# A two-layer hybrid trunk in split float32: matmuls that read and write their columns backwards, and an input tile moved to a multiple of 128 bytes

## The chip, the core and the metric

The kernel runs on one core of a Trainium2 chip. The metric is the device time of one execution in microseconds (us). One execution was also taken by the hardware profiler; all views shown here are of it. Engines: PE is TensorE's matmul side, PEld its weight load, DVE is VectorE, ACT is ScalarE, POOL is GpSimd, SP issues the DMAs.

## The reference

A decoder trunk of two layers on 256 tokens of 1024 channels, in float32. Each layer is a half-step SwiGLU FFN, a token mixer, and a second half-step FFN.

```python
h = x
for l in range(2):
    h = h + 0.5 * swiglu(rms_norm(h, ffn1_norm[l]), ffn1_w_in[l], ffn1_w_out[l])   # 1024 -> 2 x 2816 -> 1024
    u = rms_norm(h, mix_norm[l])
    (z_s, xbc, dt_s, qkv, z_d, b_d, a_d, gate_s, gate_d) = split(u @ w_in[l])      # 1024 -> 11312
    y_s = mamba2_branch(...)                # convolution, chunked state-space scan, gated norm
    y_d = deltanet_branch(...)              # convolution, chunked delta rule, gated norm
    merged = sigmoid(gate_s) * (y_s @ ssm_w_branch[l]) + sigmoid(gate_d) * (y_d @ dn_w_branch[l])
    h = h + merged @ w_out[l]
    h = h + 0.5 * swiglu(rms_norm(h, ffn2_norm[l]), ffn2_w_in[l], ffn2_w_out[l])
return rms_norm(h, final_norm)
```

## The kernel before

All large weights stream from HBM as 504 halves of 128 x 1024 floats (`load`, tile `wraw`, five buffers). ACT rounds each half to the type float32r (`whi`, line 60 through `act`), DVE subtracts (`wlo`, line 63 through `tt`); five split halves are kept. The other operand of a weight matmul is split in the same way, and a product is the sum of three matmuls in float32r: high by high, high by low, low by high. Two helpers issue those three, `mm3` (lines 208 to 211) and `mm3w` (213 to 216):

```python
PE.matmul(ps, lh, rh, start=start, stop=False)      # sum, stationary operand, moving operand
```

The second argument is the stationary operand, which is loaded into the array ahead (PEld); the third is the moving one, whose columns are streamed through; the first is the sum in PSUM, a float32 column for each moving column.

The normalised input is transposed once a norm into `uTh` and `uTl` (128 partitions, 8 blocks of 256 tokens each), high and low part. They stand in the pool `cpool`, which holds its tiles for the whole run. Weight matmuls come in three kinds:

- `chan_chunk`, by `mm3w`: the weight half is stationary (128 x 128), `uTh` or `uTl` moves with 256 columns. The sums are called `fc` in the FFNs, `kk`, `qq`, `vv`, `zd`, `bc`, `xs` in the mixer. `psm` (line 391, `scalars`) is of the same kind, with a stationary operand of 48 columns (`wsh`, `wsl`).
- `tok_chunk`, by `mm3`: a slice of `uTh` or `uTl` is stationary (128 x 128), the weight half moves with 512 columns. Sums: `f` in the FFNs, `t` in the mixer.
- `out_chunks`, by `mm3`: a slice of a split activation is stationary, the weight half moves with 512 columns. Sums: `o` (stationary `gh`, `gl` in the FFNs, `mh`, `ml` after the mixer) and `b` (stationary `bh`, `bl`, the branches).

All other matmuls (transposes, the chunked parts of the mixer) are issued directly and not through these helpers.

The order of the work is the program's order of calls (`ORDER` in the mixer) with a scheduler that places instructions by priority; the weights' order in HBM is the order in which `take` is called.

Tiles lie in SBUF one behind another within a pool. In the built program of before the tiles of `cpool` begin: `h` at byte 16512 of each partition (a multiple of 128), `cs` 24704, `mhalf` 28288, `one` 28320, `Y0` 28832, `Y1` 30880, `uTh` 32928, `uTl` 41120, `nw` 49312, `lp` 53408. So the 4-byte tile `mhalf` (with its padding 32 bytes) puts `uTh` and `uTl` 32 bytes past a multiple of 128. `wraw`, `whi`, `wlo`, `gh`, `gl`, `mh`, `ml`, `bh`, `bl` begin at multiples of 128; `wsh` and `wsl` too, with slices that begin at 0 or 64 past one.

Of the kernel before, what the change touches and what calls it, by code (L numbers as in the profile page):

```python
# [7 lines left out]
F32 = mybir.dt.float32  # L8
# [8 lines left out]
P = 128  # L17
# [8 lines left out]
LPW = 48 * 5 + 16 + 1  # L26
# [19 lines left out]
def trunk_kernel(ctx, tc, x, wst, wsm, norms, lpar, rpar, cst, out):  # L46
    nc = tc.nc
    V, A, G, PE = nc.vector, nc.scalar, nc.gpsimd, nc.tensor

    cpool = ctx.enter_context(tc.tile_pool(name="cpool", bufs=1))  # L50
# [3 lines left out]
    sm = ctx.enter_context(tc.tile_pool(name="sm", bufs=1))  # L54
# [51 lines left out]
    def ahead(key, n, fn):  # L106
        while state[key] < min(n, n_halves):
            fn(state[key])
            state[key] += 1
# [35 lines left out]
    LIMT = cs[:, 3 * P + 64 : 4 * P]  # L145
    SEL = [cs[:, 4 * P : 5 * P], cs[:, 5 * P : 6 * P]]
    LAST = cs[:, 6 * P : 7 * P]
    mhalf = cpool.tile([P, 1], F32, name="mhalf")
    V.memset(mhalf[:], -0.5)

    one = cpool.tile([1, P], F32, name="one")
# [39 lines left out]
    def norm_in(nw, add=None):  # L191

        for t in range(2):
# [4 lines left out]
            if t == 0:  # L198
# [6 lines left out]
                with tc.issue_after(ins.ins):  # L205
                    ahead("prepped", n + 2, prep)

    def mm3(ps, lh, ll, rh, rl, start, stop):
        PE.matmul(ps, lh, rh, start=start, stop=False)  # L209
        PE.matmul(ps, lh, rl, start=False, stop=False)  # L210
        PE.matmul(ps, ll, rh, start=False, stop=stop)  # L211

    def mm3w(ps, wh, wl, mh, ml, start, stop):
        PE.matmul(ps, wh, mh, start=start, stop=False)  # L214
        PE.matmul(ps, wh, ml, start=False, stop=False)  # L215
        PE.matmul(ps, wl, mh, start=False, stop=stop)  # L216

    def tok_chunk(ps, ks):

        ws = [(k, take()) for k in ks[::2]]  # L220
        for t in range(2):
            for k0, (wh, wl) in ws:
                for k in range(2):
                    kt = k0 + k
                    mm3(
                        ps[t][:],
                        uTh[:, kt, t * P : (t + 1) * P],
                        uTl[:, kt, t * P : (t + 1) * P],
                        wh[:, k * 512 : (k + 1) * 512],
                        wl[:, k * 512 : (k + 1) * 512],  # L230
                        kt == 0,
                        kt == KT - 1,
                    )

    def chan_chunk(ps):

        ws = [take(), take()]
        for a in range(2):
            for q in range(2):
                wh, wl = ws[q]  # L240
                for k in range(4):
                    kt = 4 * q + k
                    c0 = k * 256 + a * P
                    mm3w(
                        ps[:, a * 256 : (a + 1) * 256],
                        wh[:, c0 : c0 + P],
                        wl[:, c0 : c0 + P],
                        uTh[:, kt, :],
                        uTl[:, kt, :],
                        kt == 0,  # L250
                        kt == KT - 1,
                    )

    def out_chunks(ps, stat, ks, last, group=1, split=False):

        for g0 in range(0, len(ks), group):
            kk = ks[g0 : g0 + group]
            ws = [(k, take()) for k in kk]
            for t in range(2):
                order = [(k, n) for n in range(2) for k in range(len(kk))]  # L260
                if t == 1 and not split:
                    order = [(k, n) for k in range(len(kk)) for n in range(2)]
                for k, n in order:
                    k, (wh, wl) = ws[k]
                    sh, sl = stat(k, t)
                    mm3(
                        ps[t][n][:], sh, sl,
                        wh[:, n * 512 : (n + 1) * 512], wl[:, n * 512 : (n + 1) * 512],
                        k == 0, k == last,
                    )  # L270
# [58 lines left out]

    def mixer(l, nxt):  # L330
        with tc.issue_after(state["last"].ins):
            lp = cpool.tile([P, LPW], F32, tag="lp", name="lp")
            nc.sync.dma_start(lp[:], lpar[l])
            rp = cpool.tile([P, RPW], F32, tag="rp", name="rp")
            nc.sync.dma_start(rp[:], rpar[l].partition_broadcast(P))
            wsr = s2.tile([P, KT, 48], F32, tag="s2", name="wsr")
            nc.sync.dma_start(wsr[:], wsm[l])
# [51 lines left out]
        def scalars():  # L389
            psm = trb("psm")  # L390
            for kt in range(KT):
                mm3w(psm[0:48, 0:S], wsh[:, kt, :], wsl[:, kt, :], uTh[:, kt, :], uTl[:, kt, :], kt == 0, kt == KT - 1)
# [518 lines left out]
        def branch(kind, n, mk, tail=1):  # L911
            ps = [[accb("b"), accb("b")] for _ in range(2)]
            held = {}

            def stat(k, t):
                oh, ol = held[k // 2]
                return oh[:, k % 2, t * P : (t + 1) * P], ol[:, k % 2, t * P : (t + 1) * P]

            made = 1
            for j0 in list(range(n - tail)) + [n - tail]:  # L920
                js = range(j0, j0 + (tail if j0 == n - tail else 1))
                while made < min(js[-1] + 2, n):
                    mk(made)
                    made += 1
                for j in js:
                    held[j] = brT.pop((kind, j))
                out_chunks(ps, stat, [2 * j + i for j in js for i in range(2)], 2 * n - 1, group=2 * len(js))
            return ps
# [56 lines left out]
        m = tg[1]  # L985
        ps = branch("s", 8, ss_T)
        mh = slots.tile([P, KT, S], F32R, tag="sE", name="mh")
        ml = slots.tile([P, KT, S], F32R, tag="sH", name="ml")
# [26 lines left out]
    for l in range(DEPTH):  # L1015
        ffn(norm_vec(3 * l + 1))
        mixer(l, norm_vec(3 * l + 2))
        add = ffn(norm_vec(3 * l + 3) if l + 1 < DEPTH else None)
# [131 lines left out]
```

## Time and profile before

| | |
|---|---|
| median of 3 runs | 1595.85 us (1595.24 to 1600.74) |
| the profiled execution, its own time | 1593.43 us |
| its span, first to last instruction | 1591.6 us |
| granted TensorE clock | 0.999 |
| instructions | 28859, of which 11672 matmuls and as many weight loads |
| moved by DMA | 284.73 MB, mean 179 GB/s |

The profile's groups give, for each line, operation and shape, the busy time in us, the mean duration of one in ns, and the idle time of the engine before them. Matmuls overlap in the pipeline: a matmul that the groups show with 279 ns can follow the one before it after less than half of that. What a matmul costs in a dense row is therefore read from the timeline, from the start of one to the start of a later one, divided by the number of steps between them.

### The profile page before, as it was taken

To read this page: it belongs to the slowest core of one execution; us is meant where nothing else is said; L and a number is where in the kernel's file an instruction comes from. 1 tells how busy PE (TensorE), PEld (TensorE's weight loads), DVE (VectorE), ACT (ScalarE), POOL (GpSimd) and SP (SyncE) were. 2 spreads that over 40 slices of the span, in tenths; PEclk is the share of its full clock that TensorE was granted. 3 is DMA by queue.
4 is the path that set the end of the run, shared out by engine and by line. 5 is a ranking of instruction groups with operands and counts; after the bars stand their busy time and mean duration, and the time that the engine had idled before them with its cause. 6 is when DMAs were issued, how large, how long until landed. Compare 5 with 4: busy or idle time off the path is not lost.

```text
span 1591.6 us, 28859 instructions
## 1 busy us (share of the span) xinstructions
PE 1572.3 (99%) x11672; PEld 1420.9 (89%) x11672; DVE 1069.1 (67%) x1550; ACT 880.1 (55%) x1416; POOL 58.1 (4%) x60
## 2 busy tenths in 40 slices
PE   8999999999999999999999999999999999999998
PEld 7999879999888888999899987899998888889986
DVE  5555468957899766555465555698579996675554
ACT  5444468756565654444354444686656665454443
POOL 0000020000000000000000001000000000000000
PEclk9999999999999999999999999999999999999999
DMA  7555465543465456555565565655436555555562
GB/s 268 193 188 195 161 203 192 166 149 117 173 214 172 159 170 189 188 192 190 173 207 190 186 196 174 197 176 180 129 120 207 178 170 175 172 175 194 187 196 96
DMA packets 91915, 284.73 MB, mean 179 GB/s; under 512 B 22069, under 2 KB 23045, under 8 KB 90758
## 3 DMA queue, kind: packets, MB, share of 16 engines
q1 hardware_dynamic: 91782, 282.90, 54.8%
q8 instruction: 91, 1.49, 0.4%
q14 instruction: 42, 0.34, 0.1%
HBM read 280.94 MB, written 1.92 MB: 178 GB/s over the span
## 4 chain that ended last, share of the span: by engine, by line
PE 91%; DVE 4%; DMA 2%; ACT 1%; POOL 1%; issue 0%; SPq 0%; POOLq 0%; ACTq 0%
PE fc L216 9%; PE fc L214 9%; PE fc L215 9%; PE o L211 6%; PE o L209 5%; PE o L210 5%; PE t L209 4%; PE t L210 3%; PE t L211 3%; PE b L211 3%; PE b L210 2%; PE b L209 2%; PE xs L215 2%; PE xs L214 2%; PE xs L216 2%; DVE wlo L63 1%
## 5 line engine op out<-in xcount | busy, mean ns | idle before, releaser
L63 DVE TENSOR_TENSOR wlo<-wraw,whi 128x1024 fp32r<-128x1024 f32 x504 | 613.6, 1223 | 376.4 <-ACT whi L60 369.3
L60 ACT ACTIVATE whi<-wraw 128x1024 fp32r<-128x1024 f32 x504 | 531.0, 1060 | 429.3 <-PE fc L215 176.2
L214 PE MATMUL fc<-uTh,whi 128*128 128x256 f32 x1280 | 357.4, 279 | 0.0
L215 PE MATMUL fc<-uTl,whi 128*128 128x256 f32 x1280 | 357.0, 279 | 0.0
L216 PE MATMUL fc<-uTh,wlo 128*128 128x256 f32 x1280 | 357.0, 279 | 0.0
L215 PEld LDWEIGHTS fc<-uTl,whi 128*128 128x128 f32 x1280 | 240.6, 188 | 0.2
L214 PEld LDWEIGHTS fc<-uTh,whi 128*128 128x128 f32 x1280 | 240.6, 188 | 0.2
L216 PEld LDWEIGHTS fc<-uTh,wlo 128*128 128x128 f32 x1280 | 240.6, 188 | 0.0
L209 PE MATMUL o<-whi,gh 128*128 128x512 f32 x352 | 137.3, 390 | 0.0
L210 PE MATMUL o<-wlo,gh 128*128 128x512 f32 x352 | 137.3, 390 | 0.0
L211 PE MATMUL o<-whi,gl 128*128 128x512 f32 x352 | 137.0, 389 | 0.0
L209 PE MATMUL t<-whi,uTh 128*128 128x512 f32 x256 | 103.2, 404 | 1.0 <-ACT uTh L60 1.0
L210 PE MATMUL t<-wlo,uTh 128*128 128x512 f32 x256 | 101.6, 397 | 0.0
L211 PE MATMUL t<-whi,uTl 128*128 128x512 f32 x256 | 101.1, 396 | 0.0
L211 PEld LDWEIGHTS o<-whi,gl 128*128 128x128 f32 x352 | 66.1, 188 | 13.8
L210 PEld LDWEIGHTS o<-wlo,gh 128*128 128x128 f32 x352 | 66.1, 188 | 13.6
L209 PEld LDWEIGHTS o<-whi,gh 128*128 128x128 f32 x352 | 66.1, 188 | 13.4
L209 PE MATMUL b<-whi,bh 128*128 128x512 f32 x192 | 76.3, 399 | 0.0
L210 PE MATMUL b<-wlo,bh 128*128 128x512 f32 x192 | 74.9, 390 | 0.0
L211 PE MATMUL b<-whi,bl 128*128 128x512 f32 x192 | 74.3, 394 | 0.6 <-DVE bl L63 0.6
L214 PE MATMUL xs<-uTh,whi 128*128 128x256 f32 x256 | 73.1, 286 | 0.0
L216 PE MATMUL xs<-uTh,wlo 128*128 128x256 f32 x256 | 71.6, 280 | 0.0
(259 smaller groups left out, 2915.6 us busy)
## 6 DMA issues: line engine op xcount, KB each, us to landing
wraw<-in_wst_dram SPq DMA_DIRECT2D x504, 512.0 KB, 4.3
dc<-rdram SPq DMA_DIRECT2D x8, 1024.0 KB, 9.2
nw<-in_norms_dram SPq DMA_DIRECT2D x6, 512.0 KB, 4.9
gb<-rdram SPq DMA_DIRECT2D x8, 256.0 KB, 6.1
h<-in_x_dram SPq DMA_DIRECT2D x4, 256.0 KB, 3.1
out_dram<-fo SPq DMA_DIRECT2D x4, 256.0 KB, 2.3
dq<-X SPq DMA_DIRECT2D x2, 256.0 KB, 4.8
cs<-in_cst_dram SPq DMA_DIRECT2D x1, 384.0 KB, 8.2
```

The lines of the kernel that those rows point to most:

```text
L60: return A.activation(out=o, in_=i, func=func, **kw)
L63: return V.tensor_tensor(out=o, in0=a, in1=b, op=op)
L209: PE.matmul(ps, lh, rh, start=start, stop=False)
L210: PE.matmul(ps, lh, rl, start=False, stop=False)
L211: PE.matmul(ps, ll, rh, start=False, stop=stop)
L214: PE.matmul(ps, wh, mh, start=start, stop=False)
L215: PE.matmul(ps, wh, ml, start=False, stop=False)
L216: PE.matmul(ps, wl, mh, start=False, stop=stop)
```

## The change

A helper `mm` gives a matmul the same columns in reverse: the moving operand is read from its last column to its first (step -1), and the sum is written from its last column to its first, so that each column's result lands where it did. The stationary operand is read as before. All matmuls of `mm3` and `mm3w` go through it; the other matmuls stay as they are.

`mhalf` moves from `cpool` into the pool `sm`. With that, `uTh` begins at byte 32896 and `uTl` at 41088, both multiples of 128. `lp` grows from 257 to 272 columns (its DMA writes 257 as before), which takes up the 32 bytes: `rp`, `wsh`, `wsl` and all tiles of the pools for weights and activations lie where they lay. In `sm`, the small tiles move up by 32 bytes.

The order of instructions on each engine is the same in both programs, with the same DMAs.

```diff
-    mhalf = cpool.tile([P, 1], F32, name="mhalf")
+    mhalf = sm.tile([P, 1], F32, name="mhalf", bufs=1)
...
+    def mm(ps, w, m, start, stop):
+
+        PE.matmul(ps[:, ::-1], w, m[:, ::-1], start=start, stop=stop)
+
     def mm3(ps, lh, ll, rh, rl, start, stop):
-        PE.matmul(ps, lh, rh, start=start, stop=False)
-        PE.matmul(ps, lh, rl, start=False, stop=False)
-        PE.matmul(ps, ll, rh, start=False, stop=stop)
+        mm(ps, lh, rh, start, False)
+        mm(ps, lh, rl, False, False)
+        mm(ps, ll, rh, False, stop)
 
     def mm3w(ps, wh, wl, mh, ml, start, stop):
-        PE.matmul(ps, wh, mh, start=start, stop=False)
-        PE.matmul(ps, wh, ml, start=False, stop=False)
-        PE.matmul(ps, wl, mh, start=False, stop=stop)
+        mm(ps, wh, mh, start, False)
+        mm(ps, wh, ml, False, False)
+        mm(ps, wl, mh, False, stop)
...
-            lp = cpool.tile([P, LPW], F32, tag="lp", name="lp")
-            nc.sync.dma_start(lp[:], lpar[l])
+            lp = cpool.tile([P, 272], F32, tag="lp", name="lp")
+            nc.sync.dma_start(lp[:, 0:LPW], lpar[l])
```

## The prediction

> **What bounds the kernel now.** I read the busy times first, then the chain that ended last, then PE's waits, and last the timeline inside dense rows of matmuls. The first two rows are the page's busy time and its chain, the next three are the longest of PE's waits (total us, times, longest).
>
> ```profile
> PE 1572.3 (99%) x11672; PEld 1420.9 (89%) x11672; DVE 1069.1 (67%) x1550; ACT 880.1 (55%) x1416; POOL 58.1 (4%) x60
> ...
> PE 91%; DVE 4%; DMA 2%; ACT 1%; POOL 1%; issue 0%; SPq 0%; POOLq 0%; ACTq 0%
> ```
>
> ```profile
> PE hnT L184 <- DVE hn L66: 4.3, 8, 1.1
> PE nw L155 <- DMA row<-in_norms_dram: 2.3, 1, 2.3
> PE cbb L778 <- DVE vb L63: 2.0, 2, 1.6
> ```
>
> PE carries the chain and hardly waits. So the time is the sum over matmuls of the interval from one start to the next, and an edit that changes this interval by a nanosecond counts 9360 times, once for each matmul that goes through `mm3` or `mm3w`. Their numbers come from the groups by shape. I quote one of the three lines of each sum; the other two have the same count:
>
> ```profile
> L214 PE MATMUL fc<-uTh,whi 128*128 128x256 f32 x1280 | 357.4, 279 | 0.0
> L209 PE MATMUL o<-whi,gh 128*128 128x512 f32 x352 | 137.3, 390 | 0.0
> L209 PE MATMUL t<-whi,uTh 128*128 128x512 f32 x256 | 103.2, 404 | 1.0 <-ACT uTh L60 1.0
> L209 PE MATMUL b<-whi,bh 128*128 128x512 f32 x192 | 76.3, 399 | 0.0
> L214 PE MATMUL xs<-uTh,whi 128*128 128x256 f32 x256 | 73.1, 286 | 0.0
> L214 PE MATMUL zd<-uTh,whi 128*128 128x256 f32 x128 | 36.3, 284 | 0.0
> L214 PE MATMUL bc<-uTh,whi 128*128 128x256 f32 x128 | 36.3, 283 | 0.1
> L214 PE MATMUL qq<-uTh,whi 128*128 128x256 f32 x128 | 36.1, 282 | 0.0
> L214 PE MATMUL vv<-uTh,whi 128*128 128x256 f32 x128 | 35.9, 281 | 0.0
> L214 PE MATMUL kk<-uTh,whi 128*128 128x256 f32 x128 | 35.9, 281 | 0.0
> L209 PE MATMUL f<-whi,uTh 128*128 128x512 f32 x64 | 26.5, 416 | 1.3 <-ACT uTh L60 1.3
> L209 PE MATMUL o<-whi,mh 128*128 128x512 f32 x64 | 25.1, 393 | 0.0
> L214 PE MATMUL psm<-uTh,wsh 128*48 128x256 f32 x16 | 4.5, 279 | 0.0
> ```
>
> With 256 columns: 3 x (1280 + 256 + 5 x 128 + 16) = 6576, all with `uTh` or `uTl` moving. With 512 columns: 3 x (256 + 64) = 960 with `uTh` or `uTl` stationary (`t`, `f`), and 3 x (352 + 64 + 192) = 1824 with neither (`o`, `b`).
>
> Now the intervals. Each of the next fences shows a first and a last row of a dense row of matmuls on PE's timeline (start us, duration us). The first has 48 steps of `fc`, the second 24 of `o`, the third 24 of `t`:
>
> ```profile
> 59.78 0.28 PE L214 MATMUL fc<-uTh,whi 128*128 128x256 f32 x1
> ...
> 65.39 0.28 PE L214 MATMUL fc<-uTh,whi 128*128 128x256 f32 x1
> ```
>
> ```profile
> 170.18 0.39 PE L209 MATMUL o<-whi,gh 128*128 128x512 f32 x1
> ...
> 175.62 0.39 PE L209 MATMUL o<-whi,gh 128*128 128x512 f32 x1
> ```
>
> ```profile
> 208.19 0.40 PE L209 MATMUL t<-whi,uTh 128*128 128x512 f32 x1
> ...
> 213.79 0.40 PE L211 MATMUL t<-whi,uTl 128*128 128x512 f32 x1
> ```
>
> `fc`: 5.61 / 48 = 0.1169 us, over longer rows 116.7 ns for 256 columns. `o`: 5.44 / 24 = 226.7 ns for 512. `t`: 5.60 / 24 = 233.3 ns for 512. The last two are the finding of this profile. They move the same weight tiles with as many columns, and differ in the stationary operand: `gh` lies on a multiple of 128 bytes, `uTh` 32 bytes past one. So an operand 32 bytes off costs 6.7 ns a matmul, even where it is only the one that is loaded ahead. And 233.3 is twice 116.7: `fc`, whose moving operand is the one that lies off, runs at the same cost per column as `t`.
>
> **The change part by part.**
>
> *`uTh` on a multiple of 128, as a stationary operand.* 960 matmuls go from 233.3 to the 226.7 ns of `o`: 960 x 6.67 = 6.4 us. This rests on two rows of one kernel and I take it as nearly sure.
>
> *`uTh` on a multiple of 128, as a moving operand.* No row has 256 columns from an aligned tile, so this is bounded. If cost is per column, as 2 x 116.7 = 233.3 says, the aligned price is half of `o`, 113.3 ns, and 6576 x 3.33 = 21.9 us go. If instead 116.7 is a fixed part and a slope (226.7 - 116.7 = 110.0 ns for 256 further columns, which leaves 6.7 ns fixed), the moving operand's place plays no part, and the gain is 0. I take 21.9, because the exact factor of two needs no second constant.
>
> *Reading and writing backwards.* No matmul of before does it. The nearest rows are the same matmuls read forwards, so I take 0 for the direction itself. The ends: a gain down to the slope alone, 110 ns for 256 and 220 for 512 columns, that is 3.33 ns off 113.3 and 6.67 off 226.7: 6576 x 3.33 + 2784 x 6.67 = 40.5 us. As a loss I take a step of the same size, since 113.3, 116.7, 226.7 and 233.3 are all multiples of 3.33 ns: 40.5 us the other way.
>
> The width of the weight load does not matter: `psm` has a stationary operand of 48 columns where `fc` has 128, and its row shows the same 279 ns.
>
> The Trainium skill (SBUF — State Buffer, Specifications) says that SBUF is read in lines of 16 bytes and that full bandwidth needs at least two hits on a line. Four float32 columns share a line in either direction, so by that rule the direction costs nothing, as I take it; the trace shows no backward read to hold against it.
>
> *`mhalf` and `lp`.* POOL reads `mhalf` elsewhere, one DMA writes the same 257 columns into a wider tile: 0. The other engines' order does not change, so no queue has anything new in it.
>
> *What hides behind PE, and whether it holds.* The windows give the busy time of each engine in the first FFN's `fc` part, its `o` part, and the two halves of the first mixer:
>
> ```profile
> 40.00:140.00 100.00, 100.00 (x848) 99.56 (x848) 56.10 (x63) 48.24 (x63) 0.00 (x0) 1.00 0.59 188
> 150.00:190.00 40.00, 40.00 (x178) 33.13 (x177) 17.61 (x15) 14.52 (x15) 0.00 (x0) 1.00 0.59 196
> 209.00:400.00 191.00, 190.88 (x1803) 176.94 (x1802) 143.31 (x303) 128.66 (x291) 8.67 (x11) 1.00 0.51 161
> 400.00:580.00 180.00, 178.09 (x1255) 153.64 (x1254) 150.76 (x202) 110.19 (x158) 8.12 (x6) 1.00 0.53 178
> ```
>
> In `fc` a weight half feeds 24 matmuls, 24 x 116.7 = 2.80 us; with 113.3 it is 2.72 us. The `o` part already takes a half every 12 x 226.7 = 2.72 us, without a wait of PE and with DVE busy 17.6 of 40 us, so the supply holds. In the mixer DVE is busy 143 of 191 and 151 of 180 us. There 3 x (256 + 5 x 128 + 16) = 2736 short matmuls and 768 of `t` are to gain 9.1 + 5.1 = 14.2 us. If DVE were the limit in half of that stage, 7 us would turn into new waits of the transposes on DVE (`hnT`, `cbb` above are where they would grow). PE is busy 190.88 of 191 us in the first of these windows, so I subtract nothing, and keep the 7 us inside the range.
>
> **Sum.** 6.4 + 21.9 + 0 = 28.3 us. Against the profiled execution's own 1593.43 us this gives 1565.1; the median of the runs shown lies 2.4 us higher, so 1567.5, put down as 1567.
>
> **The rivals.**
>
> *Backwards is faster in itself.* Then the 110 and 220 ns are reached: 68.8 us in all, 1593.4 - 68.8 + 2.4 = 1527. For it: the matmuls stand at multiples of a 3.33 ns step, which looks like a stall that repeats along the columns and could go with a different order of reading. Against it: no row shows a matmul of this kind below the slope. Half a step more (1.67 and 3.33 ns) is another 20.2 us, 1507, and is the lowest that I allow. The Trainium skill (TensorE: Matmul & The Clock Gate, Back-to-back issue gap) gives columns / 2.4 GHz + 2.5 ns for a warm matmul, 109.2 and 215.8 ns, and by that the time would be 1510 us; forward reads in this trace do not reach it.
>
> *Only the stationary operand counts.* The fixed part and slope above, with a direction that does nothing: 6.4 us, 1589. For it: the 48-column `psm`, half of whose stationary slices lie 64 bytes off, runs like `fc`. Against it: it needs two constants that happen to give a factor of two.
>
> *Backwards is slower.* The place is the PSUM write of every one of the 9360 matmuls, or the read of its moving operand. A step of 3.33 ns for 256 columns on top of the aligned price gives 1593.4 - 28.3 + 40.5 + 2.4 = 1608. It decides from 28.3 us on, that is from 2.3 ns for 256 columns and 4.7 for 512. If each column took a second slot, 110 ns for 256 and 220 for 512 are added, 1336 us, and the kernel ends near 2900. Against it: breaks in the order of columns cost nothing visible where they come in runs; the transposes that write `oT` in runs of 64 columns with gaps take what those of `yT`, without gaps, take:
>
> ```profile
> L902 PE MATMUL yT<-cs,yz 128*128 128x128 f32 x64 | 10.2, 272 | 0.0
> ...
> L887 PE MATMUL oT<-cs,vb 128*128 128x128 f32 x32 | 4.1, 272 | 0.0
> ```
>
> The Trainium skill (PSUM — Partial Sum Buffer, Specifications) speaks for this rival: PSUM lines have 8 bytes, and any access pattern that is not contiguous slows matmuls significantly. A backward write touches the two columns of a line one after the other, and no run here says whether that counts as contiguous.
>
> **How the numbers follow.** Forecast, near 1567 (1555 to 1582): 0.35. Backwards faster in itself, 1527 and around: 0.30, of which 0.04 below 1507. Stationary operand only, near 1589: 0.13. Backwards slower: 0.22, of which 0.05 stay within 0.5% (8 us, about what a measurement of this kernel can tell from no change) because the aligned tile pays for them, 0.02 lie between that and 1608, and 0.15 above. The range runs from 1507 to 1608 and leaves out 0.04 + 0.15. Of the 1589 case 0.02 fall below 1588. Faster: 0.35 + 0.30 + 0.02 = 0.67. Same: 0.11 + 0.05 = 0.16. Slower: 0.17.
>
> **What would show it.** Right: 24 steps of `t` take 5.44 us where they took 5.60, 48 of `fc` 5.44 where they took 5.61, `o` stays at 226.7 ns, and PE's waits hardly grow. `o` and `b` lay on multiples of 128 before, so they tell of the direction alone: below 226.7 ns it gains, above it costs. `fc` still at 116.7 with `t` at 226.7 would be the rival of the stationary operand. What makes the prediction wrong is the direction: I have no row of a backward read and set it at nothing.

## The result, and the profile after

The changed kernel takes 1615.59 us (median of 4 runs, 1614.52 to 1621.44) against 1595.59 before: ratio 1.0125, 95% interval 1.0093 to 1.0158. It is slower by 20 us where 28 us less were forecast, and lies above the range. The profiled execution has a span of 1612.8 us, 21.2 more than before.

The page after, busy time and chain, and the longest of PE's waits:

```profile
PE 1594.6 (99%) x11672; PEld 1433.7 (89%) x11672; DVE 1070.4 (66%) x1550; ACT 882.7 (55%) x1416; POOL 57.6 (4%) x60
...
PE 92%; DVE 3%; DMA 2%; ACT 1%; POOL 1%; issue 0%; SPq 0%; POOLq 0%; ACTq 0%
```

```profile
PE hnT L184 <- DVE hn L66: 3.5, 6, 1.3
PE cbb L782 <- DVE vb L63: 2.4, 1, 2.4
PE nw L155 <- DMA row<-in_norms_dram: 2.3, 1, 2.3
```

Nothing new is waited for; PE is simply slower from matmul to matmul. The timeline shows it: first and last row of 48 steps of `fc`, 24 of `o`, 24 of `t`.

```profile
59.72 0.28 PE L210 MATMUL fc<-uTh,whi 128*128 128x256 f32 x1
...
65.40 0.28 PE L210 MATMUL fc<-uTh,whi 128*128 128x256 f32 x1
...
167.82 0.40 PE L210 MATMUL o<-wlo,gh 128*128 128x512 f32 x1
...
173.42 0.40 PE L210 MATMUL o<-wlo,gh 128*128 128x512 f32 x1
...
225.36 0.40 PE L210 MATMUL t<-wlo,uTh 128*128 128x512 f32 x1
...
230.96 0.40 PE L210 MATMUL t<-wlo,uTh 128*128 128x512 f32 x1
```

`fc`: 5.68 / 48 = 118.3 ns (116.7 before). `o`: 5.60 / 24 = 233.3 ns (226.7). `t`: 233.3 ns, as before. Adding up all starts to next starts in both traces: the matmuls with `uTh` and `uTl` moving take 10.2 us more, `o` and `b` 10.0 more, `t` and `f` 2.0 more (with the waits at the start of their rows), all others 1.0 less. That is the 21.2 us.

### The profile page after: what moved, and what is told of

It reads as the page before. It is cut to its first block, busy times and chain, and to the rows that moved or that the text cites. A ratio compares the mean times of both kernels' runs of the same rounds, so it can differ in the third digit from the quotient of the medians.

```text
span 1612.8 us, 28849 instructions
## 1 busy us (share of the span) xinstructions
PE 1594.6 (99%) x11672; PEld 1433.7 (89%) x11672; DVE 1070.4 (66%) x1550; ACT 882.7 (55%) x1416; POOL 57.6 (4%) x60
## 4 chain that ended last, share of the span: by engine, by line
PE 92%; DVE 3%; DMA 2%; ACT 1%; POOL 1%; issue 0%; SPq 0%; POOLq 0%; ACTq 0%
PE fc L210 28%; PE o L210 17%; PE t L210 11%; PE b L210 8%; PE xs L210 5%; PE bc L210 3%; PE vv L210 3%; PE qq L210 3%; PE kk L210 3%; PE zd L210 2%; PE f L210 2%; DMA dc<-rdram 1%; DVE wlo L63 1%; ACT whi L60 1%; PE ydb L852 1%; PE hnT L184 1%
```

## The experiments

All kernels below go by the same reading: intervals from rows of the timeline, or, where several stages are compared, the mean interval of all dense neighbours of a kind in a stage (those with a wait between them left out).

**The two halves of the change, one at a time.** First the aligned tile with forward matmuls; then backward matmuls with the tile where it was.

```diff
 (e1, against the changed kernel)
-        PE.matmul(ps[:, ::-1], w, m[:, ::-1], start=start, stop=stop)
+        PE.matmul(ps, w, m, start=start, stop=stop)
 (e2, against the kernel before: the helper mm and its calls, nothing else)
+        PE.matmul(ps[:, ::-1], w, m[:, ::-1], start=start, stop=stop)
```

> The changed kernel with forward matmuls: only uTh and uTl move to a multiple of 128 bytes. Theory A (an operand off the multiple costs per column, wherever it is): t falls from 233.3 to 226.7 ns, fc from 116.7 to 113.3, and the time to about 1567 us. Theory B (only the stationary operand's place counts): t falls to 226.7, fc stays at 116.7, about 1589. Theory C (place plays no part, and t and o differ for another reason): t 233.3, fc 116.7, 1595.

> Backward matmuls alone, uTh and uTl stay 32 bytes past the multiple. If the backward read by itself sets 233.4 ns for 512 columns and 118.4 for 256 whatever the place: 1615 us, as the changed kernel. If the place adds to it: t at about 240 ns and fc at about 121, that is 960 x 6.7 + 6576 x 2.5 = 23 us more, about 1638.

Alignment alone: 1611.45 us, ratio 1.0102 (1.0078 to 1.0125). 48 steps of `fc` and 24 of `t` in it:

```profile
59.79 0.28 PE L210 MATMUL fc<-uTh,wlo 128*128 128x256 f32 x1
...
65.55 0.28 PE L210 MATMUL fc<-uTh,wlo 128*128 128x256 f32 x1
...
225.29 0.40 PE L210 MATMUL t<-whi,uTh 128*128 128x512 f32 x1
...
230.77 0.39 PE L210 MATMUL t<-whi,uTh 128*128 128x512 f32 x1
```

`t` falls to 5.48 / 24 = 228 ns there (227.8 as the mean of the stage, most of them 226 or 227), as all but theory C said. `fc` does not fall to 113.3 and does not stay at 116.7: it rises to 5.76 / 48 = 120.0 ns. None of the three theories had that. Its price is 20.6 us over all matmuls of the kind, less 3.6 that `t` and `f` give back, by the sums of intervals in the two traces.

Direction alone: 1611.46 us, ratio 1.0094 (1.0077 to 1.0110), `fc` 117.8 ns, `o` and `t` 233.4. Nearer to the first expectation (1615) than to the second (1638). Each half alone costs some 15 us; together they cost 20, not 30. The difference comes from the matmuls with 256 columns: alignment alone costs them 20.6 us, direction alone 6.3, both together 10.2, because a backward read of the aligned tile (118.3) is cheaper than a forward one (120.0).

**Read or write.** On the aligned tile, one of the two reversed alone, so that the columns of each sum stand in reverse.

```diff
 (e3)
+        PE.matmul(ps, w, m[:, ::-1], start=start, stop=stop)
 (e4)
+        PE.matmul(ps[:, ::-1], w, m, start=start, stop=stop)
```

> Aligned tile, moving operand read backwards, sum written forwards, so each sum's columns stand in reverse and the output is not the reference's. If the read is what costs: o at 233.4 ns, fc at 118.4, as the changed kernel. If the PSUM write is: o at 226.7.

> Aligned tile, moving operand read forwards, sum written backwards (columns in reverse, output not the reference's). If the PSUM write costs: o at 233.4 ns, fc at 118.4. If the read does: o at 226.7, and fc as in the kernel with the aligned tile alone.

24 steps of `o`, of the kernel that reads backwards:

```profile
167.74 0.40 PE L210 MATMUL o<-whi,gl 128*128 128x512 f32 x1
...
173.34 0.40 PE L210 MATMUL o<-whi,gl 128*128 128x512 f32 x1
```

and of the one that writes backwards:

```profile
167.66 0.39 PE L210 MATMUL o<-whi,gh 128*128 128x512 f32 x1
...
173.10 0.39 PE L210 MATMUL o<-whi,gh 128*128 128x512 f32 x1
```

5.60 / 24 = 233.3 ns against 5.44 / 24 = 226.7. The price is the read's alone. The write is free in either direction (`fc` at 120.0 there, as with the aligned tile alone), so the rule of the Trainium skill (PSUM — Partial Sum Buffer, Specifications) that access patterns which are not contiguous slow matmuls does not reach a step of -1 here: the measurement decides.

**Place or distance.** `fc` at 120.0 with both operands on multiples of 128 speaks against a cost of being off such a multiple. A sweep gives `uTh` and `uTl` another offset in each stage (`OFF` counts elements of 4 bytes); a second kernel leaves them 32 bytes off as before and moves the weight tiles `whi`, `wlo` 32 bytes as well.

```diff
 (e5, against e1; read through a view that starts OFF elements on)
+    uTh_ = cpool.tile([P, KT * S + 128], F32R, name="uTh")
+    uTl_ = cpool.tile([P, KT * S + 128], F32R, name="uTl")
+    OFF = [16, 24, 32, 64, 4, 12]
...
 (e6, against the kernel before)
+    padA = wpool.tile([P, 8], F32, name="padA")
...
+    padB = slots.tile([P, 24], F32, name="padB")
...
```

> Forward matmuls. uTh and uTl get another place in each of the six stages between norms: 64, 96 and 128 bytes past a multiple of 512 (shared with the weight tiles) in layer 0, 256, 16 and 48 in layer 1 (FFN, mixer, FFN). What is known at 2.4 columns a ns: with moving and stationary operand at the same place mod 128 a matmul takes 32 columns' time more than its columns (226.7 and 120.0 ns), with the moving one 32 bytes ahead 24 more (116.7), with the stationary one 32 ahead 48 more (233.3). Theory distance (what counts is moving start minus stationary start, mod 128): stage 128 and stage 256 give 120.0 as at 0; 96 ahead is 32 behind, so the mixer of layer 0 has 256 columns at 126.7 ns (48 more) and t at 223.3 (24 more); 64, 16 and 48 give one steady value each. Theory period 512 or more: stage 128 or 256 differ from 120.0. Theory off or on: 16, 48, 64, 96 all give 116.7 for 256 columns and 233.3 for 512.

> The kernel before, with the weight tiles whi and wlo also 32 bytes past a multiple of 128, as uTh and uTl are; gh, gl, bh, bl, mh, ml stay on a multiple. Theory distance: fc has distance 0 and takes 120.0 ns, t 226.7, o and b have the moving operand 32 ahead and take 223.3. Theory of each operand's own place (moving off gives 24, stationary off gives 16 more): fc has both off and takes more than 116.7 by 6.7, 123.3; t has both off, about 230; o and b have the moving one off, 223.3.

48 steps of `fc` and 24 of `o` in the kernel with both moved:

```profile
59.75 0.28 PE L218 MATMUL fc<-uTh,whi 128*128 128x256 f32 x1
...
65.51 0.28 PE L218 MATMUL fc<-uTh,whi 128*128 128x256 f32 x1
...
167.69 0.39 PE L214 MATMUL o<-wlo,gh 128*128 128x512 f32 x1
...
173.32 0.40 PE L214 MATMUL o<-wlo,gh 128*128 128x512 f32 x1
```

`fc` 5.76 / 48 = 120.0 and `t` at 227.7: exactly the aligned values, although nothing is aligned. And `o`, whose `gh` stayed, rises from 226.7 to 5.63 / 24 = 234.6 (mean 234.3). So it is the distance between the two operands that counts, not where each lies; the theory of each operand's own place (123.3 and 230) falls. For `o` both theories had 223.3, and both were wrong there. The whole kernel took 1622.55 us in its one run.

Two further sweeps filled the curve:

```diff
 (e7)
+    OFF = [40, 48, 56, 20, 60, 28]
 (e10)
+    OFF = [44, 52, 36, 2, 17, 31]
```

> As the first sweep, with uTh and uTl 160, 192 and 224 bytes past in layer 0 and 80, 240 and 112 in layer 1. So far, time beyond the columns at 2.4 a ns, in columns: 256 columns moving from uTh 0, 16, 32, 48, 64, 96, 128, 256 bytes ahead of the stationary operand: 32, 25, 24, 28, 16, 32, 29, 32; 512 columns moving that many bytes behind: 32, 45, 48, 47, 48, 50, 46, about 32. Theory distance with period 256: 224 is 32 behind for 256 columns and 32 ahead for 512, and so on; if the two shapes share one curve, 224 gives 512 columns 24 (223.3 ns), 192 gives 16 (220.0), and 256 columns 48 at 224 and 192 (126.7 ns). Theory of two curves: a 512-column matmul keeps a surplus near 48 everywhere but at 0, and 256 columns stay between 16 and 32.

> Third sweep of forward matmuls: 176, 208, 144 bytes ahead in layer 0, and 8, 68, 124 in layer 1. If what counts are the 16-byte lines, 8 lies near 0 or 16 (120.0 or 116.9 ns), 68 near 64 (113.5), 124 near 112 or 128 (113.5 or 118.7). If 16 columns' time is a floor for 256 columns, no stage is below 113.3 ns; if it is not, one of them may be at 110.

Mean interval in ns of forward matmuls, by the bytes that `uTh` lies ahead of the weight tile (mod 256). For 512 columns `uTh` is the stationary operand, and some stages have only about 30 to 40 intervals of it. Most entries come from one stage of one execution.

| ahead | 256 col. | 512 col. | ahead | 256 col. | 512 col. |
|---|---|---|---|---|---|
| 0 | 120.0 | 226.7 (`o`), 227.8 (`t`) | 124 | 119.7 | 231.8 |
| 8 | 117.6 | 230.7 | 128 | 118.7 | 232.5 |
| 16 | 116.9 | 231.9 | 144 | 118.6 | 227.0 |
| 32 | 116.7 | 233.3 | 160 | 117.4 | 233.5 |
| 48 | 118.3 | 233.1 | 176 | 119.3 | 230.5 |
| 64 | 113.5 or 117.8 | 233.3 | 192 | 115.2 | 229.2 |
| 68 | 118.0 | 233.2 | 208 | 119.1 | 232.2 |
| 80 | 118.3 | 231.8 | 224 | 118.3 | 233.3 |
| 96 | 119.9 | 234.1 | 240 | 117.2 | 228.1 |
| 112 | 113.5 | 233.3 | 256 | 120.0 | 227.9 |

The curve is jagged. Distance 0 is the worst place found for 256 columns and, with 144, the best for 512. 256 gives the values of 0; nothing lies below 113.3 ns. The expectation of one curve for both shapes did not come true, and of the neighbours that were to belong together by 16-byte lines 124 (119.7) has the value of neither 112 nor 128 (68 against 64 decides nothing, since 64 has two values); 113.3 as a floor held.

Not every entry is one rate. Those at 16, 68, 96, 192, 208 and 240 come from the mixer, whose matmuls stand in many short rows. At 192 the rows of `kk` and `qq` ran at 113.3 ns and the later ones of `vv` at 117.8 in the same stage, so that 115.2 is the mean of two rates; at 16 the rows ran at 113.3, 116.7 and 118.7.

**Backward reads and distance.** The changed kernel with the tiles and views of the sweeps, and these offsets.

```diff
 (e9, backward)
+    OFF = [16, 28, 48, 0, 24, 32]
```

> Backward matmuls with uTh and uTl 64, 112 and 192 bytes ahead in layer 0 and 0, 96 and 128 in layer 1 (FFN, mixer, FFN). Known: 0 ahead 118.3 ns for 256 columns and 233.4 for 512; 32 ahead 117.8 and 233.4. Theory that a backward read sweeps past every relative place and so averages over the distance: all six stages within 117.5 to 118.5 and 233 to 234. Theory that distance counts as for forward reads: values spread as in the forward sweeps, from 113.5 to 120.

At 64, 112, 192, 0, 96 and 128 bytes: 120.0, 119.9, 117.8, 118.3, 118.0 and 120.0 ns for 256 columns, and 233.3 for 512 throughout (234.9 in the last stage, 43 intervals). The theory that a backward read averages over the distance fits 512 columns; for 256 it allowed 117.5 to 118.5 and falls by the 120.0 at three places. Read backwards, 512 columns had no good place among those tried, and 256 none below 117.8.

**A constant offset.** The best two offsets for the whole run.

```diff
 (e8 and e11: a gap of 64 bytes ahead of uTh; lp padded so that all else moves 256 or 512 bytes)
+    gap = cpool.tile([P, 16], F32, name="gap")
...
 (e12 and e13: the sweep's layout, 112 and 64 bytes ahead in every stage)
+    OFF = [28, 28, 28, 28, 28, 28]
+    OFF = [16, 16, 16, 16, 16, 16]
 (e14: 112 ahead, both parts in one tile, uTl 8192 bytes behind uTh instead of 8704)
+    both = cpool.tile([P, 2 * KT * S + 128], F32R, name="uT")
+    uTh = both[:, 28 : 28 + KT * S].rearrange("p (k t) -> p k t", k=KT)
...
```

> Forward matmuls as before, uTh and uTl 64 bytes ahead of the weight tiles' place mod 256 for the whole run (before: 32). By the sweeps, 256 columns take 113.5 ns against 116.7 and 512 columns of t and f stay at 233.3: 6576 x 3.15 = 20.7 us less, about 1575 us. If distance only shifts the cost elsewhere, as a theory that the sweeps' stages differ for other reasons would have it: 1596.

> Forward matmuls, uTh and uTl 64 bytes ahead of the weight tiles mod 512. The kernel with 64 ahead mod 256 was in fact 320 ahead mod 512 and had fc at 117.8 ns, the sweep's stage at 64 mod 512 had 113.5. Theory distance with period 512: fc 113.5, t 233.3, about 1575 us. Theory that the sweep's stage owed its value to something else (the place of uTl relative to uTh, the state in which the row of matmuls starts): fc near 117.8 and about 1599.

> Forward matmuls, the layout of the sweeps with uTh and uTl 112 bytes ahead in all six stages, as the sweep's last stage was (113.5 ns for 256 columns, 233.3 for 512). Theory distance: fc, xs and the others at 113.5 in all stages, about 1575 us. Theory that the value belongs to the state of that one execution or stage: it differs between stages or between runs, and the time is nearer to 1595.

> Forward matmuls, uTh and uTl 64 bytes ahead in all six stages in the layout of the sweeps, where uTl begins 8704 bytes behind uTh; the constant kernels with 64 ahead had 8192 and fc at 117.8 ns, the sweep's stage at 64 had 113.5. Theory that the place of uTl relative to uTh counts beside the distance: fc 113.5 in all stages, about 1580 us. Theory that the sweep's stage was the state of that stage: 117.8 in most stages, about 1600.

> Forward matmuls, 112 bytes ahead in all stages, but uTl 8192 bytes behind uTh instead of 8704. Theory that the place of uTl relative to uTh counts: fc is not at the 113.4 ns of the kernel with 8704, but steps of a column group away, 115 to 120. Theory that the distance alone counts: 113.4 again and 1580 us.

| kernel | us, median | ratio to before | `fc`, ns |
|---|---|---|---|
| 64 ahead, moved by 256 (e8) | 1599.51 | 1.0021 (1.0007 to 1.0035) | 117.8 |
| 64 ahead, moved by 512 (e11) | 1601.07 | 1.0032 (1.0019 to 1.0045) | 117.8 |
| 64 ahead, 8704 apart (e13) | 1600.36 | 1.0026 (1.0014 to 1.0038) | 117.8, one FFN 113.5 |
| 112 ahead, 8704 apart (e12) | 1580.63 | 0.9906 (0.9891 to 0.9920) | 113.5 |
| 112 ahead, 8192 apart (e14) | 1578.67 | 0.9888 (0.9868 to 0.9909) | 113.5 |

48 steps of `fc` at 112 bytes (e12), then at 64 in the first and in the second FFN of one execution (e13):

```profile
59.82 0.28 PE L218 MATMUL fc<-uTh,whi 128*128 128x256 f32 x1
...
65.26 0.28 PE L218 MATMUL fc<-uTh,whi 128*128 128x256 f32 x1
```

```profile
59.78 0.28 PE L218 MATMUL fc<-uTl,whi 128*128 128x256 f32 x1
...
65.44 0.28 PE L218 MATMUL fc<-uTl,whi 128*128 128x256 f32 x1
...
659.75 0.28 PE L218 MATMUL fc<-uTh,whi 128*128 128x256 f32 x1
...
665.19 0.28 PE L218 MATMUL fc<-uTh,whi 128*128 128x256 f32 x1
```

5.44 / 48 = 113.3 ns at 112 bytes. At 64 bytes the same program runs `fc` at 5.66 / 48 = 117.9 in one FFN and 113.3 in another: two steady rates at one distance, each held for a whole FFN. In the mixer the rate goes by the row. Two rows of `qq` in one mixer, 48 steps each, of the kernel with 64 bytes throughout (e8):

```profile
253.11 0.28 PE L212 MATMUL qq<-uTh,whi 128*128 128x256 f32 x1
...
258.76 0.28 PE L212 MATMUL kk<-uTh,whi 128*128 128x256 f32 x1
```

```profile
272.64 0.28 PE L212 MATMUL qq<-uTl,whi 128*128 128x256 f32 x1
...
278.08 0.28 PE L212 MATMUL qq<-uTl,whi 128*128 128x256 f32 x1
```

5.65 / 48 = 117.7 ns and 5.44 / 48 = 113.3. That explains why the sweep showed 113.5 and the constant kernels 117.8 for `fc`, and the place of `uTl` plays no part: at 112 both layouts give 113.5, and at 64 the sweep's own layout gives both rates. What puts a row into one or the other is open, so at some places the distance alone does not fix the interval. At 112 bytes `fc` settled at 113.3 in all four FFNs in both layouts, and most rows of the mixer did so after a slower start (mean of the stage 114.1). The two kernels with 112 bytes beat both kernels of the change, by 0.9% and 1.1% against before: in the faster one (e14) the 256-column matmuls take 17.6 us less, by the sum of intervals, and `t` and `f` 2.6 more.

## Why the prediction was wrong, point by point

*What bounds the kernel*: right. PE carries 92% of the chain, its waits did not grow, and the sum of intervals accounts for the whole 21.2 us.

*`uTh` as a stationary operand, 6.4 us off*: right in its sign in the trace of the aligned tile alone (`t` from 233.3 to 227.8; 3.6 us over `t` and `f`, which also start after waits), but by luck: not the multiple of 128 counts, as the reason given had it, and the aligned place happens to be distance 0. In the change itself the backward read took it back, and `t` is again at 233.3.

*`uTh` as a moving operand, 21.9 us off*: this step failed. Alignment alone measured 20.6 us more. I read 233.3 = 2 x 116.7 as a cost per column and set the aligned price at half of 226.7, that is 113.3. The aligned price is 120.0. At that one distance, 0, the runs have both shapes, 120.0 and 226.7 ns, and the factor of two is gone. The 256 further columns take 106.7 ns, that is 2.4 columns a ns, and what is over (the surplus, below) is 13.3 ns for either shape. At 32 bytes it is 10.0 ns for 256 columns and 20.0 for 512, which made the exact factor of two: a coincidence. The rate of 2.4 rests on one distance, and on taking the surplus of both shapes to be the same there; since it differs between them at other distances, it is not shown that a matmul pays it once, whatever its columns. Shown is that the price of 256 columns goes with the distance, and that alignment put them on their dearest place. The rejected alternative, fixed part and slope, was built on `fc` and `o`, which stood at different distances, so its slope of 110 ns is not that of one distance (106.7). The Trainium skill (TensorE: Matmul & The Clock Gate, Back-to-back issue gap) has the slope found here, columns / 2.4 GHz; its constant of 2.5 ns was not reached: the least was 113.3 - 106.7 = 6.7 ns.

*The direction, 0*: this failed too, in both signs. On the aligned tile, where a forward read stands at distance 0, a backward one costs `o` 6.7 ns a matmul and `b`, `t` and `f` 5 to 6 by the mean (10.3 us for `o` and `b`, 5.6 for `t` and `f`, between the traces of the aligned tile and the change) and saves 1.7 ns on 256 columns (10.4 us). With 0.4 us less for the others, the direction adds 5.1 us there. The bounds of one step of 3.33 ns for 256 and 6.67 for 512 columns held in the change (at 64 bytes a backward read was dearer than that: 120.0 against 113.5 or 117.8), but the range was put around an aligned price that was too low. The rule of 16-byte lines (the Trainium skill, SBUF — State Buffer, Specifications), from which the prediction took the direction to cost nothing, is not enough to tell: the lines are the same in both directions and the intervals differ.

*The rivals.* "Backwards is slower" came true in its sign, but the alignment, which no rival had as a loss, costs as much when it stands alone (some 15 us each). Its part in the PSUM write is refuted. "Backwards is faster in itself" holds only for 256 columns at 0 and 96 bytes, by 1.7 and 1.9 ns, and 118.0 and 118.3 are far from its 110. "Only the stationary operand counts" had the right doubt about the per-column reading, and the wrong rule.

What stays open: why a distance has the surplus that it has, and why some distances have two. That both reads meet somewhere fits the runs (moving both tiles together changes nothing, moving one does, turning one read round does), but no run shows where. Nor do the runs say whether the amount loaded plays a part. The prediction ruled it out by `psm`, whose stationary operand has 48 columns, but by a duration (279 ns), which is not the interval. Its mean interval was that of `fc` before (116.7 ns), and with the aligned tile alone it was 114.2 where `fc` had 120.0; its slices stand at four distances, which hides the width.

## What to carry to other kernels

In a row of dense matmuls, divide the time between two matmuls of the timeline by the number of steps and compare with columns / 2.4 in ns, the rate that distance 0 gave here; what is over is a surplus for each matmul that depends on how far the moving operand lies from the stationary one. A few bytes of padding moved it between 7 and 13 ns for 256 columns and between 13 and 21 for 512. Try some offsets and measure, over more than one row, since at some distances rows of one kernel ran at different rates, and since being on a round multiple (distance 0 for all) was here the worst place for 256 columns and among the best for 512. Two intervals that stand in a simple ratio are no evidence for a cost per column while anything else differs between the two groups.

## What the runs showed of the hardware that I had not expected

A matmul's interval depends on the relative place of its two operands (the one offset of 256 bytes that was tried gave the values of 0), from 113.3 to 120.0 ns for 256 columns and from 226.7 to 234.3 for 512. The direction of the read matters (226.7 against 233.3 ns on the same tiles), that of the write to PSUM does not. At one distance the same program can run at two steady rates, 113.3 and 117.8 ns, from row to row. The Trainium skill (TensorE: Matmul & The Clock Gate, Part 2) says that loading the next weights does not take read bandwidth from the running matmul; here the stationary operand's place changed the interval of matmuls whose moving operand and shape stayed the same: `t` went from 233.3 to 227.8 ns when its stationary operand `uTh` moved by 32 bytes.
